# Norm factors from one product of ones with the summed squares, with the root taken on all partitions

## The chip, the cores and the metric

The kernel runs on one core of a Trainium2 chip. The metric is device time in microseconds of one execution, the median over several runs of the same program.

## The reference, cut to what matters

The reference is two layers of a diffusion block on 256 tokens of x and 256 context tokens, with 1024 channels. Every layer does a half feed-forward (ffn1), a mixing part (mix) and another half feed-forward (ffn2); the context leaves the last layer after mix's projections. Each of the three begins with a norm over the channels, and a last norm follows the second layer.

```python
def rms_norm(x, g):
    xf = x.astype(jnp.float32)
    y = xf * lax.rsqrt(jnp.mean(xf * xf, axis=-1, keepdims=True) + EPS)
    return (y * g.astype(jnp.float32)).astype(x.dtype)

def modulate(h, shift, scale):
    return h * (1 + scale) + shift

def half_ffn(h, shift, scale, gate, g, wi, wo):
    return h + 0.5 * gate * swiglu(modulate(rms_norm(h, g), shift, scale), wi, wo)
```

The convolution branch of mix has a layer norm over its 256 channels, which takes a sum of squares and a root in the same way.

## The kernel before, in words

Everything stays in fp32. A weight product of two fp32 matrices is written as three products of rounded parts (mm3, L177 to L179): high by high, high by low and low by high. So each weight tile `raw` that a DMA brings is split into `whi` (a cast on ScalarE, L165) and `wlo` (the difference on VectorE, L166), and each activation into a high part (`yh`, `hh`, `mh`) and a low part (`yl`, `hl`, `ml`). There are two buffers each of whi and wlo, and four PSUM tiles (`psm`) for the weight products and four (`psa`) for the small ones.

x lies in eight tiles of 128 channels by 512 tokens, of which columns 0 to 255 are x and 256 to 511 the context. The channels are on partitions, so a norm's sum over channels is a sum over partitions and over the eight tiles. It is made up of these steps:

- sumsq: ScalarE squares a tile of x (L374), VectorE adds it to the running sum `ss` (L378). The eighth tile's square is kept by itself.
- rstd: for each 128 tokens two fp32 products with `mean` as the moving side (L391 with ss, L392 with the last square) put the mean on the partitions, one column for each 128 tokens. An fp32 product shows as two records in the profile. rsqrt_cols (L204 to L215) takes the root of these columns with three Newton steps on VectorE.
- spread and bcast: VectorE multiplies the identity with each column (`diag`, L225), and a product with `ones` (L227) puts the factor of every token on all partitions, in a psa tile.
- norm_scale (L416) makes `ny` from x, the gain and that psa tile; norm_shift adds the shift on ScalarE, which gives yh (L423), and makes yl on VectorE (L424).

The output projection of each part ends in `project`. Where x and the context are both there, its last two output tiles (m = 6 and 7) are held back and then done by token halves: tile 6 first half, tile 7 first half, tile 6 second half, tile 7 second half. Each ends in x's update (L479) and sumsq. During the second half, hooks put rstd of the first half (at RA eighths of the products of tile 6) and its spread (at RB eighths of tile 7) among the weight products, so that the next part's norm of the first half is under way while TensorE works. There are four such places, with 256 tokens in each half.

In the last layer's ffn2 only x is left. There the first two weight pairs are multiplied with x times the gain, before the norm's factor is known (`z`), and late_act (L541) multiplies the results by the factor `rb` afterwards (zg at L544, zv at L546), which frees their psm tiles.

A tile scheduler sets the order of each engine's instructions from priorities, which follow the order of the code, and from a model of when operands are ready; each engine then works through its list in order. The start of the program (up to the first weight products) is ordered by the code as written. Waits between engines are by semaphore.

## Time and profile before

| what | value |
|---|---|
| runs | 1703.88, 1705.18, 1705.04 us (median 1705.04) |
| profiled execution, its own time | 1703.85 us |
| its span | 1702.1 us |
| mean granted TensorE clock | 0.997 of full speed |
| TensorE busy | 1678.8 us (99%) |
| VectorE busy | 1193.8 us (70%) |
| ScalarE busy | 575.8 us (34%) |

The span runs from the first to the last instruction of the profiled execution. A busy share says how much of the span an engine had an instruction in work. TensorE's instructions are pipelined: a product of 128x256 is recorded with 0.28 us, but at full clock they start 0.12 us apart. The granted clock is the share of full speed that the throttle gave TensorE. In the rows an engine, a line of the kernel and the operation are followed by what is written and what is read, without buffer numbers, and in brackets by the idle time before it and what ended that.

### The profile page before, as it was taken

How to read it: one execution, taken by the hardware profiler on the slowest of the kernel's cores; microseconds unless marked ns; L12 is line 12 of the kernel's file. 1: busy time of each engine (PE TensorE's matmuls, PEld its weight loads, DVE VectorE, ACT ScalarE, POOL GpSimd, SP SyncE). 2: the span in 40 equal slices, each digit the busy share in tenths (PEclk: the TensorE clock that was granted, in tenths of full speed). 3: DMA queues.
4: the chain of work that ended last, by engine and by line, in shares of the span. 5: the costliest groups of instructions: out<-in, count | busy, mean ns of one | idle time of the engine just before them, and what ended most of it. 6: DMA issues, size and time to landing. Idle time of an engine off the chain costs nothing.

```text
span 1702.1 us, 23539 instructions
## 1 busy us (share of the span) xinstructions
PE 1678.8 (99%) x9650; PEld 1440.4 (85%) x9650; DVE 1193.8 (70%) x2077; ACT 575.8 (34%) x737; POOL 33.6 (2%) x59
## 2 busy tenths in 40 slices
PE   8999999999999999999999999999999998999998
PEld 5888888878888898888888898888878897899998
DVE  5799866896675678888669776654464678775555
ACT  3322212333532443222122242221233254554343
POOL 0000000010000000000000000000000000000010
PEclk9999999999999999999999999999999999999999
DMA  9555644533232235545445425444433234344552
GB/s 370 185 188 182 211 157 153 180 121 104 102 105 85 95 129 180 183 163 183 166 148 193 165 104 194 166 155 149 151 124 106 86 130 162 110 157 177 179 195 79
DMA packets 51452, 262.55 MB, mean 154 GB/s; under 512 B 6010, under 2 KB 10944, under 8 KB 28816
## 3 DMA queue, kind: packets, MB, share of 16 engines
q1 hardware_dynamic: 49968, 257.05, 42.9%
q0 software_dynamic: 1376, 4.00, 0.6%
q8 instruction: 75, 1.23, 0.3%
q14 instruction: 33, 0.27, 0.0%
HBM read 257.88 MB, written 3.15 MB: 153 GB/s over the span
## 4 chain that ended last, share of the span: by engine, by line
PE 92%; DVE 3%; DMA 2%; ACT 1%; issue 1%; SPq 0%; POOL 0%; DVEq 0%; ACTq 0%; POOLq 0%
PE psm L177 29%; PE psm L178 28%; PE psm L179 28%; DVE acc L316 1%; ACT whi L165 1%; DVE wlo L166 1%; DMA adaw<-in_ada_w_dram 1%; DMA pm<-in_k_pool_dram 1%; PE psa L979 1%; DMA vec<-in_vecs_dram 1%; PE psa L1216 0%; PE psa L1038 0%; PE psa L1198 0%; PE psa L331 0%; PE psa L881 0%
## 5 line engine op out<-in xcount | busy, mean ns | idle before, releaser
L179 PE MATMUL psm<-yh,wlo 128*128 128x512 f32 (+1 forms) x1616 | 570.1, 354 | 2.5 <-DVE wlo L166 2.5
L177 PE MATMUL psm<-yh,whi 128*128 128x512 f32 (+1 forms) x1616 | 570.3, 355 | 1.4 <-DVE glu L776 0.9
L178 PE MATMUL psm<-yl,whi 128*128 128x512 f32 (+1 forms) x1616 | 571.1, 354 | 0.1
L165 ACT CAST whi<-raw 128x2048 fp32r<-128x2048 f32 (+3 forms) x172 | 304.1, 1770 | 599.8 <-PE psm L178 534.6
L166 DVE TENSOR_TENSOR wlo<-raw,whi 128x2048 fp32r<-128x2048 f32 (+3 forms) x172 | 363.7, 2116 | 133.6 <-ACT whi L165 133.3
L179 PEld LDWEIGHTS psm<-yh,wlo 128*128 128x128 f32 x1616 | 305.5, 189 | 46.5 <-DVE wlo L166 4.0
L177 PEld LDWEIGHTS psm<-yh,whi 128*128 128x128 f32 x1616 | 304.6, 189 | 46.3 <-issue 3.1
L178 PEld LDWEIGHTS psm<-yl,whi 128*128 128x128 f32 x1616 | 305.7, 189 | 42.5 <-DVE yl L424 0.9
L316 DVE SCALAR_TENSOR_TENSOR acc<-adaw,cvec,acc 128x512 f32<-128x512 f32 x392 | 274.5, 746 | 2.8
L177 PE MATMUL psm<-hh,whi 128*128 128x512 f32 (+1 forms) x752 | 265.1, 353 | 0.0
L179 PE MATMUL psm<-hh,wlo 128*128 128x512 f32 (+1 forms) x752 | 264.4, 352 | 0.0
L178 PE MATMUL psm<-hl,whi 128*128 128x512 f32 (+1 forms) x752 | 264.3, 351 | 0.0
L178 PEld LDWEIGHTS psm<-hl,whi 128*128 128x128 f32 x752 | 142.3, 189 | 19.4 <-DVE hl L166 0.4
L179 PEld LDWEIGHTS psm<-hh,wlo 128*128 128x128 f32 x752 | 142.3, 189 | 19.4 <-DVE acc L316 0.8
L177 PEld LDWEIGHTS psm<-hh,whi 128*128 128x128 f32 x752 | 142.2, 189 | 18.7 <-issue 0.2
L496 DVE TENSOR_TENSOR sg<-psm,sg 128x512 f32<-128x512 f32 (+1 forms) x90 | 54.3, 605 | 133.6 <-PE psm L179 119.6
L479 DVE SCALAR_TENSOR_TENSOR x<-psm,gt,x 128x256 f32<-128x256 f32 x112 | 50.4, 478 | 115.9 <-PE psm L179 115.8
L495 ACT ACTIVATE sg<-psm 128x512 f32<-128x512 f32 (+1 forms) x90 | 47.9, 532 | 215.7 <-PE psm L179 215.7
L374 ACT ACTIVATE sq<-x 128x512 f32<-128x512 f32 (+1 forms) x64 | 33.2, 523 | 90.9 <-DVE x L479 74.7
L177 PE MATMUL psm<-whi,yh 128*128 128x256 f32 (+1 forms) x200 | 58.1, 295 | 0.6 <-ACT whi L165 0.6
L178 PE MATMUL psm<-wlo,yh 128*128 128x256 f32 (+1 forms) x200 | 58.1, 294 | 0.0
L179 PE MATMUL psm<-whi,yl 128*128 128x256 f32 (+1 forms) x200 | 57.9, 293 | 0.0
(287 smaller groups left out, 1480.9 us busy)
## 6 DMA issues: line engine op xcount, KB each, us to landing
raw<-in_ffn_wi_dram SPq DMA_DIRECT2D x88, 1024.0 KB, 4.8
adaw<-in_ada_w_dram SPq DMA_DIRECT2D x66, 1024.0 KB, 5.1
raw<-in_ffn_wo_dram SPq DMA_DIRECT2D x32, 896.0 KB, 4.6
raw<-in_ffn_wo_dram SPq DMA_DIRECT2D x16, 1024.0 KB, 5.0
raw<-in_w_in_dram SPq DMA_DIRECT2D x14, 1024.0 KB, 4.8
raw<-in_w_out_dram SPq DMA_DIRECT2D x8, 1024.0 KB, 4.9
adaw<-in_ada_w_dram SPq DMA_DIRECT2D x24, 256.0 KB, 7.2
pm<-in_k_pool_dram SPq DMA_DIRECT2D x12, 256.0 KB, 3.1
```

The costliest lines, as they stand in the source:

```text
L165: self.nc.scalar.copy(hi[:, s], src[:, s])
L166: self.nc.vector.tensor_tensor(lo[:, s], src[:, s], hi[:, s].bitcast(F32), op=ALU.subtract)
L177: mm(ps, lhsT=ah, rhs=bh, start=first, stop=False)
L178: mm(ps, lhsT=ah, rhs=bl, start=False, stop=False)
L179: mm(ps, lhsT=al, rhs=bh, start=False, stop=last)
L316: nc.vector.scalar_tensor_tensor(acc, ws[half][:, k, :], sc, acc, op0=ALU.mult, op1=ALU.add)
L374: nc.scalar.activation(sq, self.x[m][:, lo:lo + n], AF.Square)
L479: nc.vector.scalar_tensor_tensor(self.x[m][:, s], ps[:, v * S - lo:v * S - lo + S], gate[v][:, m:m + 1], self.x[m][:, s], op0=ALU.mult, op ...
L495: nc.scalar.activation(sg, w[2][:, s], AF.Silu)
L496: nc.vector.tensor_tensor(sg, w[3][:, s], sg, op=ALU.mult)
L979: nc.tensor.matmul(ps[par], lhsT=fwd[:, 2 * i + par, :], rhs=cur[par], start=True, stop=True)
```

## The change

The eighth square is now added to ss like the others. For each half of 256 tokens one fp32 product of ones with ss puts the sum on all partitions, in a psa tile of 128x256. The root is then taken on that tile by eleven operations on VectorE, of which the last writes the factor back into the psa tile. Column products, diagonals and the products that spread them are gone from these norms; the last norm of the program keeps its columns, with one product for each 128 tokens. The factor no longer holds the square root of 1024, so the norms' gains are multiplied by it once at the start. The ones product of a first half is issued in the hook at RA; the hook at RB is gone, and the second half's follows its last weight product. In the convolution branch the two squares are added on VectorE, and one column product for each 128 tokens is left of two.

```diff
--- before.py
+++ after.py
@@ -35,7 +35,7 @@
 PRE = 400
 FSPLIT = 14
 F0 = (2.0, 0, 0.8, 16)
-RA, RB = 2, 4
+RA = 2
 PZ = 2
 F1 = (1.9, 0, 1)
 F2 = (0.8, 0, 1.0, 20)
@@ -240,6 +240,7 @@
                 v[name] = vt[:, l, at:at + c]
                 at += c
             self.vec.append(v)
+        self.norms = vt[:, :, 72:96]
 
 
     def ada_init(self, craw):
@@ -374,30 +375,37 @@
         nc.scalar.activation(sq, self.x[m][:, lo:lo + n], AF.Square)
         if m == 0:
             self.ss, self.rb = sq, {}
-        elif m < KT - 1:
+        else:
             nc.vector.scalar_tensor_tensor(self.ss[:, lo:lo + n], sq, EPS * D / P if m == 1 else 0.0, self.ss[:, lo:lo + n],
                                            op0=ALU.add, op1=ALU.add)
-        else:
-            self.last_sq = sq
 
     def rstd(self, lo, n):
 
         nc = self.nc
-        sq = self.last_sq
         nt = n // P
         ps = self.pa((P, nt, 2))
         for j in range(nt):
             a = lo + j * P
-            nc.tensor.matmul(ps[:, j, :], lhsT=self.ss[:, a:a + P], rhs=self.mean, start=True, stop=False)
-            nc.tensor.matmul(ps[:, j, :], lhsT=sq[:, j * P:j * P + P], rhs=self.mean, start=False, stop=True)
+            nc.tensor.matmul(ps[:, j, :], lhsT=self.ss[:, a:a + P], rhs=self.mean, start=True, stop=True)
         self.r = self.rsqrt_cols(ps, nt)
         return self.r
 
-    def spread(self, lo, r):
-
-        for i in range(r.shape[1] * P // S):
-            c = i * S // P
-            self.rb[lo // S + i] = self.bcast(r[:, c:c + S // P], S // P)
+    def spread(self, lo, n):
+
+
+        nc = self.nc
+        for v in range(lo // S, (lo + n) // S):
+            ps = self.pa((P, S))
+            nc.tensor.matmul(ps, lhsT=self.ones, rhs=self.ss[:, v * S:v * S + S], start=True, stop=True)
+            t = self.tmp((P, 2, S), name="root")
+            a, y = t[:, 0, :], t[:, 1, :]
+            nc.vector.tensor_single_scalar(a.bitcast(I32), ps.bitcast(I32), 1, op=ALU.logical_shift_right)
+            nc.vector.tensor_scalar(y.bitcast(I32), a.bitcast(I32), -1.0, float(0x5F3759DF), op0=ALU.mult, op1=ALU.add)
+            for i in range(3):
+                nc.vector.tensor_tensor(a, y, y, op=ALU.mult)
+                nc.vector.scalar_tensor_tensor(a, a, -0.5, ps, op0=ALU.mult, op1=ALU.mult)
+                nc.vector.scalar_tensor_tensor(ps if i == 2 else y, a, 1.5, y, op0=ALU.add, op1=ALU.mult)
+            self.rb[v] = ps
 
     def norm(self, l, name, T):
         yh = [self.yp.tile([P, T], F32R, tag="y", name=self.nm("yh")) for _ in range(KT)]
@@ -452,19 +460,11 @@
         elif m == KT - 2:
             self.held = (m, wh, wl, act, gate)
         else:
-            state = {}
-
-            def stats():
-                state["r"] = self.rstd(0, S)
-
-            def spread():
-                self.spread(0, state["r"])
-
             self.part(*self.held, 0, S, 3)
             self.part(m, wh, wl, act, gate, 0, S, 3)
-            self.part(*self.held, S, S, 3, {len(act) * RA // 8: stats})
-            self.part(m, wh, wl, act, gate, S, S, 3, {len(act) * RB // 8: spread})
-            self.spread(S, self.rstd(S, S))
+            self.part(*self.held, S, S, 3, {len(act) * RA // 8: lambda: self.spread(0, S)})
+            self.part(m, wh, wl, act, gate, S, S, 3)
+            self.spread(S, S)
 
     def part(self, m, wh, wl, act, gate, lo, w, last, hooks={}):
         nc = self.nc
@@ -480,10 +480,10 @@
                                            self.x[m][:, s], op0=ALU.mult, op1=ALU.add)
         if last:
             self.sumsq(m, lo, w)
-            if m == KT - 1 and last < 3:
-                r = self.rstd(lo, w)
-                if last == 1:
-                    self.spread(lo, r)
+            if m == KT - 1 and last == 1:
+                self.spread(lo, w)
+            elif m == KT - 1 and last == 2:
+                self.rstd(lo, w)
 
     def up_tiles(self, T):
         wh, wl = self.whl((P, 2 * KT, P))
@@ -921,17 +921,16 @@
         for i in range(2):
             nc.tensor.matmul(mu, lhsT=self.ones, rhs=cacc[i], start=i == 0, stop=i == 1)
         yield
-        sqs = []
+        sqs = self.tmp((P, T), name="css")
         for i in range(2):
             nc.vector.scalar_tensor_tensor(cacc[i], mu, -1.0 / DG, cacc[i], op0=ALU.mult, op1=ALU.add)
-            sq = self.tmp((P, T), name="csq")
+            sq = sqs if i == 0 else self.tmp((P, T), name="csq")
             nc.scalar.activation(sq, cacc[i], AF.Square)
-            sqs.append(sq)
+        nc.vector.tensor_tensor(sqs, sqs, sq, op=ALU.add)
         n = T // P
         ps = self.pa((P, n))
         for j in range(n):
-            for i in range(2):
-                nc.tensor.matmul(ps[:, j:j + 1], lhsT=sqs[i][:, j * P:(j + 1) * P], rhs=self.ones[:, 0:1], start=i == 0, stop=i == 1)
+            nc.tensor.matmul(ps[:, j:j + 1], lhsT=sqs[:, j * P:(j + 1) * P], rhs=self.ones[:, 0:1], start=True, stop=True)
         yield
         rb = self.bcast(self.rsqrt(ps, n, 1.0 / DG), n)
         for i in range(2):
@@ -1271,7 +1270,7 @@
             self.warm_up()
             for m in range(KT):
                 self.sumsq(m, 0, 512)
-            r = self.rstd(0, 512)
+            self.spread(0, 512)
             yh = [self.yp.tile([P, 512], F32R, tag="y", name=self.nm("yh")) for _ in range(KT)]
             yl = [self.yp.tile([P, 512], F32R, tag="y", name=self.nm("yl")) for _ in range(KT)]
             up = [self.up_tiles(512) for _ in range(2)]
@@ -1300,8 +1299,8 @@
                 self.split(up[i][0][:, half[p]], up[i][1][:, half[p]], raws[i][:, half[p]])
 
             acc = [self.pa() for _ in range(2)]
+            nc.vector.tensor_scalar(self.norms, self.norms, D ** 0.5, None, op0=ALU.mult)
             self.gemv(ws[2], every, acc[0])
-            self.spread(0, r)
             self.ada_end(0, 2, self.ada_row(acc[0]))
             self.derive(0, [1], two, 0, 4)
             scale(first)
```

The scheduler sets new orders with this. VectorE at B, the place where layer 0's mix ends and its ffn2 begins (about 616 to 622 us), before; sm, diag and psa_5218 belong to the root of the first half, x_113 to x_120 are the eight tiles of x, wlo is the low part of ffn2's second weight tile:

```order
L215 SCALAR_TENSOR_TENSOR sm_903_5178<-sm_902_5177,sm_901_5172 128x1
L225 TENSOR_SCALAR diag_5219<-ident_99,sm_903_5178 128x128 x2
L378 SCALAR_TENSOR_TENSOR sq_4920<-sq_5202,sq_4920 128x256
L416 SCALAR_TENSOR_TENSOR ny_5290<-x_113,gs_2817,psa_5218 128x256
L416 SCALAR_TENSOR_TENSOR ny_5294<-x_114,gs_2817,psa_5218 128x256
L416 SCALAR_TENSOR_TENSOR ny_5298<-x_115,gs_2817,psa_5218 128x256
L424 SCALAR_TENSOR_TENSOR yl_5282<-ny_5290,mods_197,yh_5274 128x256
L479 SCALAR_TENSOR_TENSOR x_120<-psm_5205,mods_197,x_120 128x256
L416 SCALAR_TENSOR_TENSOR ny_5302<-x_116,gs_2817,psa_5218 128x256
L166 TENSOR_TENSOR wlo_5365<-raw_5370,whi_5364 128x1024
```

and at the same place now, where root and psa_5085 are the first half's root and psa_5150 the second half's sums; the new lines L402 to L407 are the root, L379 is the sum of squares and L424 is norm_scale:

```order
L379 SCALAR_TENSOR_TENSOR sq_4850<-sq_5118,sq_4850 128x256
L406 SCALAR_TENSOR_TENSOR root_5087<-root_5087,psa_5085 128x256
L407 SCALAR_TENSOR_TENSOR root_5087<-root_5087 128x256
L405 TENSOR_TENSOR root_5087<-root_5087 128x256
L479 SCALAR_TENSOR_TENSOR x_120<-psm_5121,mods_197,x_120 128x256
L406 SCALAR_TENSOR_TENSOR root_5087<-root_5087,psa_5085 128x256
L166 TENSOR_TENSOR wlo_5255<-raw_5260,whi_5254 128x1024
L407 SCALAR_TENSOR_TENSOR psa_5085<-root_5087 128x256
L379 SCALAR_TENSOR_TENSOR sq_4850<-sq_5147,sq_4850 128x256
L424 SCALAR_TENSOR_TENSOR ny_5180<-x_113,gs_2790,psa_5085 128x256
L424 SCALAR_TENSOR_TENSOR ny_5184<-x_114,gs_2790,psa_5085 128x256
L402 TENSOR_SCALAR root_5152<-psa_5150 128x256
```

The norm_scales stood ahead of x_120 and of the split of wlo; now they stand behind both, and the root's last operation stands behind the split.

TensorE at B now, from the last weight product of the held tiles (mh by wlo) on; yh_5164 is the first of ffn2's eight yh tiles:

```order
L179 MATMUL psm_5121<-mh_4813,wlo_5015 128x256
L399 MATMUL psa_5150<-sq_4850,ones_100 128x256
L177 MATMUL psm_5246<-yh_5164,whi_5244 128x256
L177 MATMUL psm_5247<-yh_5164,whi_5244 128x256
L177 MATMUL psm_5256<-yh_5164,whi_5254 128x256
L177 MATMUL psm_5257<-yh_5164,whi_5254 128x256
L178 MATMUL psm_5246<-yl_5172,whi_5244 128x256
```

Behind the second half's ones product the list goes on with products that all read yh, as it did before behind a column product of the second half.

VectorE at E, the norm ahead of the last layer's ffn2 (about 1511 us), before; psm_12493 and psm_12494 hold the results of the first unscaled weight pair, wlo_12744 belongs to a later weight tile:

```order
L424 SCALAR_TENSOR_TENSOR yl_12457<-ny_12483,mods_198,yh_12449 128x256
L424 SCALAR_TENSOR_TENSOR yl_12458<-ny_12487,mods_198,yh_12450 128x256
L544 TENSOR_TENSOR zg_12592<-psm_12493,rb_12518 128x256
L546 TENSOR_TENSOR zv_12593<-psm_12494,rb_12518 128x256
L166 TENSOR_TENSOR wlo_12744<-raw_12749,whi_12743 128x2048
```

and now, where L432 is norm_shift's low part:

```order
L424 SCALAR_TENSOR_TENSOR ny_12276<-x_120,gs_9892,psa_12194 128x256
L166 TENSOR_TENSOR wlo_12533<-raw_12538,whi_12532 128x2048
L432 SCALAR_TENSOR_TENSOR yl_12245<-ny_12268,mods_198,yh_12237 128x256
L544 TENSOR_TENSOR zg_12381<-psm_12282,rb_12307 128x256
L432 SCALAR_TENSOR_TENSOR yl_12246<-ny_12272,mods_198,yh_12238 128x256
L546 TENSOR_TENSOR zv_12382<-psm_12283,rb_12307 128x256
```

The split moved from behind zg and zv to ahead of both.

## Rows read from the trace of the kernel before

**Rows 1.** The page, busy time: engine, us (share of the span), instructions.

```profile
PE 1678.8 (99%) x9650; PEld 1440.4 (85%) x9650; DVE 1193.8 (70%) x2077; ACT 575.8 (34%) x737; POOL 33.6 (2%) x59
```

**Rows 2.** Windows A and B: us; busy PE, PEld, DVE, ACT, POOL; clock; DMA.

```profile
410.00:422.00 12.00, 11.10 (x75) 10.48 (x73) 10.11 (x35) 5.92 (x11) 1.19 (x3) 0.86 0.31 105
618.00:630.00 12.00, 11.94 (x98) 11.50 (x97) 11.40 (x38) 6.42 (x12) 0.00 (x0) 1.00 0.00 1
```

**Rows 3.** Timeline of TensorE at B: start, us, engine, instruction.

```profile
613.68 0.38 PE L392 MATMUL psa<-mean,sq 128*128 128x2 f32 x2
...
614.38 0.36 PE L178 MATMUL psm<-ml,whi 128*128 128x256 f32 x1
...
617.57 0.61 PE L227 MATMUL psa<-diag,ones 128*128 128x128 f32 x4
617.93 0.36 PE L177 MATMUL psm<-mh,whi 128*128 128x256 f32 x1
...
619.60 0.48 PE L177 MATMUL psm<-yh,whi 128*128 128x256 f32 x2
```

**Rows 4.** Timelines of ScalarE (first row) and VectorE at B.

```profile
613.21 0.42 ACT L374 ACTIVATE sq<-x 128x256 f32<-128x256 f32 x1 [0.95 <-DVE x L479]
...
614.55 0.16 DVE L204 TENSOR_SCALAR sm<-psa 128x2 int32<-128x2 int32 x1 [1.43 <-PE psa L392]
...
618.22 1.26 DVE L416 SCALAR_TENSOR_TENSOR ny<-x,gs,psa 128x256 f32<-128x256 f32 x3 [0.26 <-PE psa L227]
...
620.62 1.22 DVE L166 TENSOR_TENSOR wlo<-raw,whi 128x1024 fp32r<-128x1024 f32 x1
```

**Rows 5.** Groups of TensorE: instructions | busy us, mean ns | idle before.

```profile
L934 PE MATMUL psa<-ones,csq 128*128 128x1 f32 x24 | 2.9, 240 | 0.0
...
L650 PE MATMUL psa<-abs,ones 128*128 128x256 f32 x8 | 2.6, 404 | 0.0
```

**Rows 6.** Groups of VectorE, shapes apart.

```profile
L314 DVE TENSOR_SCALAR acc<-adaw,cvec 128x512 f32<-128x512 f32 x56 | 26.1, 480 | 0.0
...
L652 DVE TENSOR_SCALAR rinv<-psa 128x256 f32<-128x256 f32 x4 | 1.7, 424 | 2.3 <-PE psa L650 2.3
```

**Rows 7.** Timeline of VectorE, two operations of which the second needs the first.

```profile
1284.81 0.42 DVE L682 TENSOR_TENSOR sp<-sp,psa 128x256 f32<-128x256 f32 x1 [3.23 <-ACT sp L681]
1285.27 0.42 DVE L684 TENSOR_TENSOR sp<-sp,psa 128x256 f32<-128x256 f32 x1
```

**Rows 8.** Windows of one microsecond at A.

```profile
414.00:415.00 1.00, 0.96 (x7) 0.96 (x7) 1.00 (x2) 1.00 (x3) 0.00 (x0) 0.78 0.00 0
415.00:416.00 1.00, 1.00 (x6) 1.00 (x6) 1.00 (x6) 0.19 (x1) 0.00 (x0) 0.50 0.00 0
...
417.00:418.00 1.00, 1.00 (x6) 1.00 (x6) 1.00 (x6) 0.51 (x1) 0.00 (x0) 0.52 0.85 344
```

**Rows 9.** Timelines of TensorE and VectorE at A.

```profile
411.77 0.36 PE L177 MATMUL psm<-yh,whi 128*128 128x256 f32 x1
...
412.89 2.33 DVE L166 TENSOR_TENSOR wlo<-raw,whi 128x1152 fp32r<-128x1152 f32 x2
...
414.92 0.56 PE L177 MATMUL psm<-yh,whi 128*128 128x256 f32 x1
```

**Rows 10.** Timelines of VectorE, ScalarE and TensorE at E.

```profile
1511.42 0.42 DVE L544 TENSOR_TENSOR zg<-psm,rb 128x256 f32<-128x256 f32 x1
1511.61 1.91 ACT L165 CAST whi<-raw 128x2048 fp32r<-128x2048 f32 x1 [0.37 <-ACT rb L563]
1511.75 0.41 DVE L546 TENSOR_TENSOR zv<-psm,rb 128x256 f32<-128x256 f32 x1
1511.89 0.39 PE L177 MATMUL psm<-yh,whi 128*128 128x256 f32 x1 [0.25 <-DVE zg L544]
...
1513.55 2.29 DVE L166 TENSOR_TENSOR wlo<-raw,whi 128x2048 fp32r<-128x2048 f32 x1 [1.38 <-ACT whi L165]
```

**Rows 11.** Timeline of VectorE at the start.

```profile
34.51 0.23 DVE L293 TENSOR_TENSOR mods<-psa,vec 128x4 f32<-128x4 f32 x2 [5.72 <-PE psa L291]
```

## The prediction

> **What bounds the kernel now.** The busy shares come first: TensorE works for 99% of the span, VectorE for 70% [rows 1]. So a product that leaves TensorE is worth its own time, and work on VectorE costs nothing until TensorE waits for it. Windows over the places where a norm ends one product and starts the next come second. At four of them the last two output tiles are done half by half: A at 410 us (ffn1 to mix, layer 0), B at 618 (mix to ffn2), C at 986 (ffn2 to ffn1 of layer 1), D at 1360 (ffn1 to mix, layer 1). At B TensorE is busy for 11.94 of 12 us at full granted clock; at A, where a longer weight split is in the way, for 11.10 at 0.86 [rows 2]. C reads like B, D like A. A fifth norm, E (mix to ffn2, layer 1), stands at 1496 to 1512: there the first two weight pairs work on unscaled x, and the scale is put on their results.
>
> Third, the timelines of B, where the reader is to see how a norm is hidden. TensorE's last column product for the first half is through at 614.38 [rows 3]; VectorE starts the root at 614.55 and the norm_scales at 618.22, after the diagonals and their products [rows 4]. TensorE meanwhile works on the second half of the held tiles and takes its first product with yh at 619.60 [rows 3]. The norm's chain takes 3.7 us and its cover is about 5 us; what the change does to these two numbers decides.
>
> **Removed and added on TensorE.** Of a half's eight records of column products at B, the last six run from 613.68 to 614.38, 0.70 us, which is 0.93 for eight at that pace; the first two are issued ahead among weight products, so I take 0.85. Its diagonal products hold TensorE from 617.57 to 617.93, 0.36 us [rows 3]. In their place comes one fp32 product of 128x256: L650's eight records, two for each product, take 2.6 us [rows 5], so 0.65. Net -0.55 per half. In the conv branch half of L934's 2.9 us goes [rows 5], and one 256-wide add on VectorE comes: -1.2, bounds -1.5 and 0.
>
> **The root.** Before, L204 to L215 work on two columns. Now eleven operations work on 128x256, each on the result of the one before. The nearest rows: a 256-wide operation that reads PSUM takes 424 ns [rows 6]; two that depend on each other start 0.46 us apart [rows 7]; two that don't, 0.33 apart (zg to zv) [rows 10]. L403, one integer input, isn't shown; L314, one input of 512 columns, takes 480 ns [rows 6], and half of that and the dependent price are its bounds: I take 0.32. With the others at 0.45 the chain is 4.8 us, between 3.6 (all at 0.33) and 5.1 (all at 0.46). I take the dependent price because every operation waits for its predecessor.
>
> **B, step by step.** The last square of the first half ends at 613.63 [rows 4]; its add (0.42, a third of three norm_scales' 1.26 [rows 4]) ends at 614.1, the ones product at 614.75. Ten root operations follow (4.4 us), and between them VectorE's list has three others (x of the last two tiles, one square's add, 0.4 each): 620.4. Then the weight split L166 stands ahead of the last root operation, where before four norm_scales stood ahead of it. It takes 1.22 [rows 4]: 621.6. The last root operation, a square's add and the first norm_scale end at 622.7, ScalarE's yh at 623.25, and the first product with yh starts at 623.3 instead of 619.60 [rows 3]. Nothing can fill the gap: the next rows on TensorE's list all read yh, and behind them stands all the rest. That is +3.7. Off it goes what the second half no longer does behind that point, 0.85 + 0.4 (its ones product falls into the wait): +2.45.
>
> **The clock.** At A the profile shows what a hold-up brings. TensorE is stopped there for a moment by the long split, and the granted clock is 0.78 in the microsecond from 414 and 0.52 in that from 417 [rows 8], with 0.50 between: half speed (1.2 GHz) from about 414.6 to 417.95, while TensorE was busy with six records in each microsecond. Half of these 3.35 us is lost, 1.7. At B nothing of the kind was there before [rows 2], and a wait of 4 us (619.1 to 623.3), longer than A's, now comes. I add 1.7: B +4.1, and C the same. The Trainium skill has this as a rule (TensorE: Matmul & The Clock Gate, Part 1): an array left idle falls to 1.2 GHz and must be busy for a while before it has 2.4 again. It speaks against this change, and A's rows agree; were the wait alone the price, the sum below would be 5 us less.
>
> **A and D.** The same list, with two splits of together 2.33 us [rows 9]: first product with yh at about 416.25 instead of 411.77. But before did little from there: three products with yh and two behind the first cast, 0.9 us, and its next block came at 414.92 [rows 9], with the slow clock behind it. So 416.25 - 414.92, plus 0.9 that is now still to do, less the second half's diagonals with their gaps (0.5): +1.7 each; the clock falls in both kernels.
>
> **E.** VectorE's list now has zg of the first unscaled pair behind the split of a later weight tile. zg frees the PSUM tile for TensorE's next product, which started at 1511.89, after a wait of 0.25 for it [rows 10]. Now the cast on ScalarE (1.91) starts when the second unscaled pair is done, about 0.65 sooner than 1511.64; then the split of 2.29 [rows 10], one norm_shift and zg: 1511.0 + 1.9 + 0.1 + 2.3 + 0.8 = 1516.1. That is +4.2, and with the clock +5.9.
>
> **The rest.** At the start the roots and the scaling of the gains are some 4.5 us more on VectorE, which idles for 5.72 us before 34.51, behind them [rows 11]. I take that idle time as their cover: 0, and +4.5 if the work that ends it is late by as much. The final norm keeps its columns, has one add in front and two products fewer: +0.25.
>
> **Sum** on the profiled run (1703.85 us, 1.75 of it around the span): 2 x 4.1 + 2 x 1.7 + 5.9 - 1.2 + 0.25 = +16.55, or 1720.4. The median of the runs shown, 1705.04, is 1.2 above that run: 1721.5.
>
> **Rivals.**
> 1. The other side. The products that go are the gain and the roots stay hidden: eleven halves at -0.55 and -1.2 in the conv branch, -7, so 1698. For it: TensorE at 99%. It turns on one number: at B the time from the sums (614.75) to yh must stay under the 4.4 us until the second half's products end at 619.1. Against it: at the lowest price the root is 3.6, and a norm_scale, yh and the split come on top. Steps under 0.28 us and a split behind the last of them would be needed.
> 2. The waits come, the clock does not fall for B, C and E: -5.1, 1716.5. For it: at E TensorE's wait of 0.25 left no mark. Against it: A.
> 3. The slow clock lasts twice as long at all five places, since the second half's eleven root operations stand among the first half's norm_scales and may break the stretch again (twelve products are 1.5 us of TensorE, 98 records in 12 us [rows 2], one norm_scale and shift 0.8 of VectorE): + 5 x 1.7, 1730.
> 4. Waits and gains cancel: within 0.2% (3.4 us, about what a measurement of this kernel tells from no change), 1705. It needs the split to move behind the root and E's wait to vanish.
>
> **Chances.** Forecast 0.62, rival 2 0.14, rival 3 0.10, rival 1 0.08, rival 4 0.06. The range goes down to rival 2 with roots at the independent price (1.2 us at each of five places, and the conv branch at its best): 1709; up to rival 3 and the start's bound in part: 1731. Faster is rival 1, 0.08; same rival 4 and a little of rival 2's lower end, 0.07; slower 0.85.
>
> **What would show it.** In the profile after: L402 to L407 in steps of 0.45; at B and C TensorE without work for about 4 us and a granted clock near 0.8 in the window that had 1.00; the split between the last two root operations; at E zg behind the split. The forecast is wrong, and rival 1 right, if the steps are near 0.3 or TensorE is still busy for 11.9 us of the window at B; rival 2 is right if TensorE waits and the clock stays at 1.00.

## The result, and the profile after

The changed kernel takes 1722.37 us (median of 4 runs, 1722.09 to 1723.12) against 1704.59 for the kernel before: the ratio is 1.0102, 95% interval 1.009 to 1.0114. It is slower by 17.8 us. Forecast were 1721.5. The total is right, in part because errors cancel; of the reasons behind it, the price of the slow clock was wrong and the one for E was half of the story. The experiments show both.

The profile after. Its page, busy times and the chain that ended last (for the first see [rows 1]):

```profile
PE 1678.8 (98%) x9524; PEld 1434.8 (83%) x9524; DVE 1220.0 (71%) x2028; ACT 576.3 (33%) x737; POOL 33.6 (2%) x59
...
PE 89%; DVE 6%; DMA 2%; ACT 2%; issue 1%; SPq 0%; DVEq 0%; ACTq 0%
```

TensorE's busy time is the same to a tenth although 126 records are gone, and the span is 18.6 us longer: some of its work ran at half speed, and for some microseconds it stood still. What it waited for (total us, times, longest), the first two lines of its list of waits:

```profile
PE psa L399 <- DVE sq L379: 14.5, 6, 4.2
PE psm L177 <- DVE zg L544: 5.0, 1, 5.0
```

Neither stood in the list of before. The first is the second half's ones product at A (4.16), B (2.95), C (2.95) and D (4.16), which waits for the last square's add; the second is E. The root's operations:

```profile
L405 DVE TENSOR_TENSOR root<-root 128x256 f32<-128x256 f32 x33 | 13.9, 422 | 0.7
...
L407 DVE SCALAR_TENSOR_TENSOR psa<-root 128x256 f32<-128x256 f32 x11 | 4.7, 426 | 0.1
...
L402 DVE TENSOR_SCALAR root<-psa 128x256 int32<-128x256 int32 x11 | 4.6, 421 | 4.5 <-PE psa L399 4.5
...
L403 DVE TENSOR_SCALAR root<-root 128x256 int32<-128x256 int32 x11 | 3.2, 290 | 0.2
```

They last 0.42 us each and 0.29 for L403. The timeline of VectorE at B shows the steps of 0.46 and 0.32, and the weight split between the last two root operations:

```profile
617.50 0.42 DVE L402 TENSOR_SCALAR root<-psa 128x256 int32<-128x256 int32 x1 [0.79 <-PE psa L399]
617.96 0.29 DVE L403 TENSOR_SCALAR root<-root 128x256 int32<-128x256 int32 x1
618.28 0.43 DVE L405 TENSOR_TENSOR root<-root 128x256 f32<-128x256 f32 x1
...
622.25 0.41 DVE L406 SCALAR_TENSOR_TENSOR root<-root,psa 128x256 f32<-128x256 f32 x1
622.64 1.22 DVE L166 TENSOR_TENSOR wlo<-raw,whi 128x1024 fp32r<-128x1024 f32 x1
623.79 0.43 DVE L407 SCALAR_TENSOR_TENSOR psa<-root 128x256 f32<-128x256 f32 x1
624.12 0.42 DVE L379 SCALAR_TENSOR_TENSOR sq<-sq,sq 128x256 f32<-128x256 f32 x1
624.46 0.86 DVE L424 SCALAR_TENSOR_TENSOR ny<-x,gs,psa 128x256 f32<-128x256 f32 x2
```

Where before had 3.67 us from the first root operation to the first norm_scale [rows 4], it is 6.96 now. TensorE at B, and one-microsecond windows of the same place (us; busy PE, PEld, DVE, ACT, POOL; granted clock; DMA):

```profile
624.60 0.70 PE L399 MATMUL psa<-sq,ones 128*128 128x256 f32 x2 [2.95 <-DVE sq L379]
625.53 0.74 PE L177 MATMUL psm<-yh,whi 128*128 128x256 f32 x4 [0.23 <-ACT yh L431]
```

```profile
622.00:623.00 1.00, 0.00 (x0) 0.00 (x0) 1.00 (x3) 1.00 (x3) 0.00 (x0) 1.00 0.00 0
...
627.00:628.00 1.00, 1.00 (x6) 1.00 (x6) 1.00 (x4) 0.49 (x1) 0.00 (x0) 0.50 0.00 0
...
629.00:630.00 1.00, 1.00 (x8) 1.00 (x8) 1.00 (x4) 0.00 (x0) 0.00 (x0) 0.68 0.00 0
```

The reader is to see three things: nothing on TensorE at 622, half the clock behind the wait, and VectorE at 1.00 in every row. The third is the one that the forecast used only in a rival. At E, ScalarE, VectorE and TensorE (before: [rows 10]):

```profile
1522.68 1.90 ACT L165 CAST whi<-raw 128x2048 fp32r<-128x2048 f32 x1 [0.96 <-PE psm L178]
...
1524.61 2.29 DVE L166 TENSOR_TENSOR wlo<-raw,whi 128x2048 fp32r<-128x2048 f32 x1 [0.70 <-ACT whi L165]
...
1524.90 0.35 ACT L563 COPY rb<-psa 128x256 f32<-128x256 f32 x1
...
1527.22 0.42 DVE L544 TENSOR_TENSOR zg<-psm,rb 128x256 f32<-128x256 f32 x1
...
1527.69 0.58 PE L177 MATMUL psm<-yh,whi 128*128 128x256 f32 x1 [4.97 <-DVE zg L544]
```

To put the loss down to places, each weight split (wlo) and each activation product (sg) of a kernel was set beside the same one of the kernel before; its start less the one of before is the shift there. The step of a place is the median shift behind it less the one ahead of it, in us, one profiled execution of each kernel; E's is taken from the splits just ahead of it (1480 to 1494), behind layer 1's convolution branch:

| kernel | start | A | B | C | D | E | median of runs |
|---|---|---|---|---|---|---|---|
| changed | 1.85 | 1.66 | 3.25 | 4.23 | 1.47 | 6.86 | 1722.4 |
| e_zg | 1.69 | 1.91 | 3.08 | 3.10 | 1.89 | 4.88 | 1721.7 |
| e_rb | 1.27 | 1.75 | 3.05 | 3.08 | 1.89 | 2.93 | 1717.3 |
| e_order | 1.17 | 1.52 | 2.95 | 2.95 | 1.54 | 7.63 | 1720.8 |
| e_two | 2.54 | 0.46 | 4.34 | 4.36 | 0.93 | 6.44 | 1720.9 |
| e_clock | 1.68 | 2.03 | 5.97 | 5.99 | 2.00 | 6.71 | 1728.7 |
| e_half | 3.41 | 2.17 | 3.89 | 2.76 | 1.92 | 6.31 | 1722.7 |
| e_clock1 | -0.06 | 2.00 | 2.86 | 2.92 | 1.96 | 6.57 | 1721.5 |
| e_both | 2.54 | 0.05 | 1.72 | 1.74 | 0.28 | 7.45 | 1715.9 |
| e_cols | 3.48 | -0.72 | 3.81 | 3.82 | 0.07 | 0.21 | 1711.3 |
| e_win | 1.80 | 0.16 | 0.51 | 0.49 | 1.63 | 0.19 | 1704.2 |
| e_sqrt | 1.32 | 3.04 | 5.55 | 5.27 | 2.11 | 1.46 | 1725.4 |
| e_conv | 3.15 | -1.47 | 0.00 | -0.02 | -1.52 | 0.00 | 1702.8 |

Two places stand between these. Where the convolution branch of layer 0 is (between the splits at 565 and 590), the changed kernel gains 0.89, and so does every other kernel of the table. Where layer 1's is (1449 to 1481), it gains 0.40 and e_conv 0.30, the others between 0 and 0.72; ahead of that, from 1418 to 1426, the changed kernel loses 0.34, of which the cause was not followed up.

One execution is not the next, and this has to be kept in mind with every step. e_zg and e_rb have the changed kernel's code and lists at A to D, and there C's step is 3.1 in both and not 4.23. The kernels from e_zg to e_both but e_two have the changed kernel's start, and e_conv has that of the kernel before, yet their starts lie between -0.06 and 3.41, and 3.15. That goes with the clock of the single execution: over 24 to 48 us it is 1.00 in the kernel before and in e_clock1 (start -0.06), 0.93 in the changed kernel and e_zg (1.85, 1.69) and 0.86 in e_half and e_conv (3.41, 3.15).

### The profile page after: what moved, and what is told of

It is laid out like the page before. It is cut to its first block, busy times and chain, and to the rows that moved or that the text cites. A ratio compares the mean times of both kernels' runs of the same rounds, so it can differ in the third digit from the quotient of the medians.

```text
span 1720.7 us, 23239 instructions
## 1 busy us (share of the span) xinstructions
PE 1678.8 (98%) x9524; PEld 1434.8 (83%) x9524; DVE 1220.0 (71%) x2028; ACT 576.3 (33%) x737; POOL 33.6 (2%) x59
## 3 DMA queue, kind: packets, MB, share of 16 engines
HBM read 257.88 MB, written 3.15 MB: 152 GB/s over the span
## 4 chain that ended last, share of the span: by engine, by line
PE 89%; DVE 6%; DMA 2%; ACT 2%; issue 1%; SPq 0%; DVEq 0%; ACTq 0%
PE psm L177 28%; PE psm L178 28%; PE psm L179 28%; DVE wlo L166 1%; DVE acc L317 1%; ACT whi L165 1%; DMA adaw<-in_ada_w_dram 1%; DMA vec<-in_vecs_dram 1%; PE psa L1037 0%; PE psa L1215 0%; PE psa L978 0%; DMA pm<-in_k_pool_dram 0%; PE psa L399 0%; PE psa L1197 0%; PE psa L332 0%
```

## The experiments

**E alone.** e_zg holds VectorE's order at E, e_rb also ScalarE's:

```diff
 def up(f, pieces=1):
     w = self.up_tiles(T)
-    self.split(w[0], w[1], self.load(wi[f]), pieces)
+    with self.after({**self.late[0], **self.copied} if early and f > 2 else {}):
+        self.split(w[0], w[1], self.load(wi[f]), pieces)
```

Here `late[0]` is VectorE's zv of the first unscaled pair, `copied` is ScalarE's copy of rb (e_rb only), and `after` queues the block's instructions behind them on the same engine.

> The changed kernel with one edit: in the last layer's ffn2 the split of the fourth weight tile is queued on VectorE behind zv of the first unscaled pair, so zg comes first, as before the change. Theory (zg behind the split stops TensorE at E, the wait 5.0 us and the half clock behind it): about 6.9 us of the 17.8 come back, 1715.5 us, no wait of TensorE for zg over 0.5 us and a granted clock of 1.00 from 1518 to 1537. Rival (TensorE would there wait for the weight tile or for yl instead, so the wait only changes its name): 1721 to 1723.

> The changed kernel with its orders at E as before the change, on both engines: on ScalarE the copy of the norm factor (rb) stands ahead of the cast of the fourth weight tile, on VectorE zg and zv ahead of its split. In e_zg, with VectorE's order alone, zg waited for rb, which stood behind the cast. Theory (the cast of 1.9 us and the split of 2.3 in a row are E's price, with the half clock behind the wait): the shift between the two kernels' rows over E falls from 6.85 us to about 0.5, 1716 us or 2 below e_zg. Rival (E's norm is late by itself, as the root on VectorE ends 2.4 us later than before): it falls to 3 only.

e_zg: 1721.71 us, ratio to before 1.0101 (1.0084 to 1.0118); TensorE still waits 3.2 us for zg. ScalarE in e_zg says why:

```profile
1522.28 1.90 ACT L165 CAST whi<-raw 128x2048 fp32r<-128x2048 f32 x1 [0.96 <-PE psm L178]
...
1524.49 0.35 ACT L566 COPY rb<-psa 128x256 f32<-128x256 f32 x1
```

zg needs rb, and rb's copy stands behind the cast. E's step falls by 2.0. e_rb: 1717.34, ratio 1.0076 (1.006 to 1.0091), with rb ahead of the cast:

```profile
1522.26 0.37 ACT L566 COPY rb<-psa 128x256 f32<-128x256 f32 x1 [0.46 <-DVE ny L424]
1522.88 0.42 DVE L546 TENSOR_TENSOR zg<-psm,rb 128x256 f32<-128x256 f32 x1
...
1523.35 0.39 PE L177 MATMUL psm<-yh,whi 128*128 128x256 f32 x1 [2.38 <-DVE zg L546]
```

E's step falls from 6.86 to 2.93, to the rival's 3 and not to the theory's 0.5: two orders, on two engines, make 3.9 us of it. The rest is put down to a norm that is late by itself, which no kernel tests alone.

**The split between the root's operations.** e_order queues the split at A to D behind the third norm_scale:

```diff
+            with self.after(self.behind if pieces > 1 else {}), self.prio(-PRE if pieces > 1 else 0):
                 self.nc.vector.tensor_tensor(lo[:, s], src[:, s], hi[:, s].bitcast(F32), op=ALU.subtract)
```

> The changed kernel with one edit: at the four half-by-half boundaries the weight split that stood between the last two root operations is queued on VectorE behind the third norm_scale. Theory (VectorE's list with the root, the split and the norm_scales in a row is what TensorE waits for): the waits shrink by the split's length, 1.2 us at B and C and 2.3 at A and D, 7 us in all: 1715.4 us, and down to 1709 if shorter waits leave the clock up. Rival (TensorE needs the split's low part as soon as yh, so its products with wlo wait instead): 1720 to 1726.

1720.76, ratio 1.0095 (1.008 to 1.011). The four steps together fall from 10.6 to 9.0 (e_zg and e_rb, with the split in its old place, have 10.0 and 9.8), not by 7. The first yh comes sooner and later ones come late: in e_order TensorE waits 6.5 us for yh, in six pieces. The place of the split was not the price, and the time is in the rival's range.

**A shorter root.** e_two has two Newton steps:

```diff
-            for i in range(3):
+            for i in range(2):
```

> The changed kernel with two Newton steps in the root in place of three (the third step is left out, so the norm factors are less exact): eight operations in the chain instead of eleven, 1.37 us less, and the scheduler then puts the weight split behind the root and the norm_scales at B. Theory (the root's length on VectorE goes one to one into TensorE's wait): at B and C the wait falls from 3.9 to about 1 us and the clock stays up, 4.5 us each; A and D 3 to 4 each, the start 1.5: 1705 to 1710. Rival (TensorE's waits come from elsewhere, or something else is late next): 1718 to 1723.

1720.9, ratio 1.0096 (1.0079 to 1.0112): in the rival's range and not the 1705 to 1710 of the theory. At A and D the steps fall by 1.2 and 0.5, at B they rise by 1.1. At B and C the scheduler put the second piece of the split behind all norm_scales, a second difference, and e_cols and e_win below show that this one alone costs 3.3 us at each of the two.

**The clock alone, and VectorE's work alone.** e_clock keeps TensorE busy in the wait; e_half leaves the second half's root out:

```diff
             self.part(m, wh, wl, act, gate, S, S, 3)
-            self.spread(S, S)
+            with self.after(self.mark(mybir.EngineType.PE)):
+                ps = self.pa((P, P))
+                for i in range(16):
+                    self.nc.tensor.matmul(ps, lhsT=self.ones, rhs=self.ones, start=True, stop=True)
+                with self.after(self.mark(mybir.EngineType.PE)):
+                    self.spread(S, S)
```

```diff
+            if lo:
+                self.rb[v] = self.rb[0]
+                continue
             t = self.tmp((P, 2, S), name="root")
```

> The changed kernel with one edit: at the four half-by-half boundaries 16 products of ones with ones (128x128, result unused) stand on TensorE's list between the last held weight product and the second half's ones product, that is in the wait. Theory (the wait lets the clock fall, and the half-speed stretch behind it is a price of its own): with the clock at 1.00 through and behind the wait, the lost time by the windows' granted clocks, (1 - 0.77) x 15 at A and C and (1 - 0.89) x 15 at B and D, comes back, 10 us: 1712; by the forecast's 1.7 for each of four places, 1715.6. Rival (the slow stretch has another cause, the wait is the whole price): 1722 or somewhat above.

> The changed kernel without the root of the second half at the four half-by-half boundaries; the context tokens there take the factors of the first half's tokens (the roots left out are the second half's alone, its sums are still made and waited for). The first half's chain keeps its eleven operations and, by the order of VectorE's list, the split in front of the last. Theory T (VectorE is busy without a gap from the sums to the last norm_scale, and its whole work there paces TensorE): B and C lose most of their 3.3 and 4.4 us, 1715 us. Theory L (the forecast's: the time to the first yh and the clock behind it are the price): the first half's chain is as long as before, 1721 to 1723.

e_clock: 1728.72, ratio 1.0143 (1.0127 to 1.0159), slower than the changed kernel although its clock stays up. e_half: 1722.74, ratio 1.0107 (1.0094 to 1.0121), as the changed kernel. By e_half theory T fell, by e_clock the forecast's price for the clock. But e_clock's lists differ at B and C as e_two's do, and e_half's there have the split's second piece further ahead, behind the third norm_scale. At A and D the splits stand in all of them where they do in the changed kernel. So the pair was run again in one order.

At B the record has a plainer case against that price. The changed kernel and e_zg have the same code and the same lists there; in the one execution the clock fell behind the wait, in the other it did not (columns as in [rows 2], the changed kernel first):

```profile
618.00:634.00 16.00, 12.82 (x89) 12.07 (x88) 15.82 (x42) 6.34 (x12) 0.00 (x0) 0.89 0.01 2
```

```profile
618.00:634.00 16.00, 12.57 (x99) 11.62 (x97) 15.79 (x42) 6.25 (x12) 0.00 (x0) 1.00 0.01 2
```

The steps are 3.25 and 3.08 (e_rb, also at 1.00: 3.05), so this fall cost 0.2 us and not 1.7. VectorE was full in both. At C the fall lasted longer in the changed kernel than in e_zg (granted clock 0.79 and 0.89 over 990 to 1006), and there the steps are 4.23 and 3.10: a longer fall has a price.

**Both together.** e_both has both edits, e_clock1 the products alone, and both queue the second piece of the split ahead of the second half's norm_scales at B and C (the branch for these tiles; all others are split as before):

```diff
+                self.split(w[0][:, :KT], w[1][:, :KT], raw[:, :KT])
+                nc.scalar.copy(w[0][:, KT:], raw[:, KT:])
+                with self.after(self.eighth), self.prio(-PRE):
+                    nc.vector.tensor_tensor(w[1][:, KT:], raw[:, KT:], w[0][:, KT:].bitcast(F32), op=ALU.subtract)
```

> e_clock and e_half together (16 products of ones with ones in each of the four waits, and no root of the second half, which takes the first half's factors), with the split's second piece at B and C ahead of the second half's norm_scales as in the changed kernel. Theory P (behind the first yh two limits run side by side, TensorE at half clock and VectorE's full list, so that taking away either alone gave nothing): with both away the boundaries cost only the wait for the first yh, some 2 us less at each of the four: about 1714 us. Theory L (the wait for the first yh alone is the price): 1722. If the products in the wait cost time by themselves, as e_clock's 1728.7 may be read: 1726 or above.

> e_clock with the split's second piece at B and C queued ahead of the second half's norm_scales, as in the changed kernel and in e_both: so it is e_both with the second half's root put back. Theory P (with the clock up, VectorE's full list is the limit behind the first yh): the steps at B and C come to the changed kernel's 3.3 to 4.2 us, from e_clock's 6.0, and 1.5 us or more above e_both's 1.7; A and D stay at 2.0: 1722 to 1724 us. Rival (the second half's root plays no part, e_both gained by the order alone): the steps at B and C come to 1.7, A and D to 0.1 to 0.3: 1716.

e_both: 1715.88, ratio 1.0064 (1.005 to 1.0078). e_clock1: 1721.47, ratio 1.0097 (1.0083 to 1.0111). Sixteen microseconds at A show it, first the changed kernel, then e_half, e_clock1 and e_both (columns as in [rows 2]):

```profile
412.00:428.00 16.00, 11.84 (x73) 11.00 (x72) 15.81 (x41) 7.24 (x14) 1.19 (x3) 0.79 0.23 80
```

```profile
413.70:429.70 16.00, 11.84 (x68) 10.92 (x67) 13.81 (x33) 8.89 (x19) 0.00 (x0) 0.79 0.23 76
```

```profile
412.00:428.00 16.00, 14.16 (x99) 12.32 (x98) 15.62 (x39) 7.33 (x19) 0.00 (x0) 1.00 0.22 75
```

```profile
412.00:428.00 16.00, 15.18 (x119) 14.35 (x117) 15.21 (x37) 9.29 (x19) 0.00 (x0) 1.00 0.22 76
```

With the root taken away, VectorE has 2 us free and TensorE's clock is as low as before the edit (0.79): nothing gained. With the clock at 1.00, VectorE is full (15.62), and TensorE waits for it behind the first yh, as e_clock1's waits in this window say (yh is made on ScalarE from ny, which comes from VectorE's list). e_clock1 is 1.9 us ahead of the changed kernel here; from 410.1 on its row has 15.85 for VectorE and the same clock.

```profile
PE psm L177 <- ACT yh L433: 1.3, 3, 0.5
PE psa L399 <- DVE sq L379: 0.6, 1, 0.6
```

With both, A's step is 0.05 and D's 0.28, from 2.0 and 2.0 with the clock alone and 2.2 and 1.9 with the root alone. The 16 products stand in e_both too, so it is not they that cost e_clock1 its 2 us. So behind the wait two limits run side by side, TensorE at half speed and VectorE's full list, of about the same length here; taking one away shows the other. That is theory P, and A and D show it. At B and C only part of P came: e_clock1's steps are 2.9 and e_both's 1.7, so the root does count with the clock up, but by 1.1 to 1.2 and not by the 1.5 or more that P asked for, and 2.9 is under its 3.3 to 4.2.

The 0.05 doesn't say that the wait is free. The kernel before ran at half the clock for a while at A and D itself [rows 8], and e_conv, whose clock stayed up there, is 1.5 us faster at each. Counted from a kernel with its clock up, e_both's wait costs about 1.5 at A and 1.8 at D, as the 1.7 at B and C, and the two limits together 1.2 to 1.6 more at each place of the changed kernel, 2.5 at C with its longer fall. These are estimates from the steps of single executions.

**Parts of the change on the kernel before.** e_cols takes the eighth add with half the column products, and the convolution branch, and keeps the narrow root and E's orders; e_win adds the second piece's place (as in e_both) and eight products at the start; e_conv has the convolution branch alone:

```diff
-            nc.tensor.matmul(ps[:, j, :], lhsT=self.ss[:, a:a + P], rhs=self.mean, start=True, stop=False)
-            nc.tensor.matmul(ps[:, j, :], lhsT=sq[:, j * P:j * P + P], rhs=self.mean, start=False, stop=True)
+            nc.tensor.matmul(ps[:, j, :], lhsT=self.ss[:, a:a + P], rhs=self.mean, start=True, stop=True)
```

> The kernel before with its column products, diagonals and narrow roots, and two parts of the change taken alone: the eighth square is added on VectorE, so a half has two column products instead of four, and the convolution branch has one column product for each 128 tokens instead of two; the orders at E are held as in the kernel before. Theory: TensorE loses 0.4 us a half and 0.8 to 1.2 in the convolution branch, 11 halves, 5 in all; VectorE gets one more 256-wide add a half, which at B and C, where it has no gap, gives 0.8 each back: 1700.5 us, below the kernel before (1704.0). Rival (the adds are hidden): 1699; rival (they stand in front of the root in a chain that has no room): 1704 or above.

> e_cols with two more edits: at B and C the second piece of the second weight tile's split is queued on VectorE behind the eighth norm_scale of the first half and ahead of the second half's, as in the kernel before (in e_cols it stood behind all norm_scales), and at the start eight products of ones with ones, result overwritten, fill TensorE's gap at 28 to 30 us. Theory (e_cols lost at B and C by that order, 2.1 us each and waits behind it, and at the start by the clock, 3.5 us): B and C come to -0.8 each, the start to 0, the convolution branch -0.8 and A, D, E near 0: 1701.5 us, below the kernel before (1704.5). Rival (the eighth add delays the second half's sums and TensorE waits all the same): 1707 or above; rival (the start's clock does not heed eight products): 1705.

> The kernel before with the convolution branch's part of the change alone (its two squares added on VectorE, one column product for each 128 tokens instead of two); the lists of the engines are else as before. Theory (the forecast's -1.2 us, 0.8 and 0.4 in the two layers): 1.0 to 1.4 us below the kernel before; by the rows of the changed kernel, where the shift falls by 0.9 in layer 0 and rises by 0.4 in layer 1, 0.5. Rival (TensorE has other work there, nothing is gained): no difference.

e_cols: 1711.28, ratio 1.0039 (1.0026 to 1.0051), 11 us above its theory: it lost 3.8 at B and at C with no wide root in it, and 3.5 at the start. The wait that ends the stretch there, TensorE in e_cols, and ten microseconds of e_cols and then of e_win:

```profile
638.80 0.50 PE L179 MATMUL psm<-yh,wlo 128*128 128x256 f32 x2 [0.52 <-DVE wlo L166]
```

```profile
634.00:644.00 10.00, 8.65 (x61) 7.42 (x61) 6.75 (x16) 3.75 (x8) 0.00 (x0) 1.00 0.30 105
```

```profile
634.00:644.00 10.00, 10.00 (x84) 9.94 (x83) 6.28 (x17) 6.00 (x11) 0.00 (x0) 1.00 0.08 34
```

In e_cols the split's second piece runs at 637.53 on VectorE, in e_win at 629.41. With that order set, e_win's steps at B and C are 0.5 (not the -0.8 that was expected) and its time is 1704.15, ratio 0.9989 (0.998 to 0.9998). e_conv: 1702.76, ratio 0.9986 (0.9977 to 0.9995). Both are below the kernel before by about 0.1%, their intervals overlap, and the rest of the change brought no gain beyond e_conv's in any form that was run. e_conv's own part is its 0.89 in layer 0 and 0.30 in layer 1, 1.2 together. Its profile's further gain at A and D (1.5 each) comes with a clock of 1.00 from 412 to 420, where the kernel before ran three microseconds at half speed [rows 8], and why that differs between two kernels with the same code there stays open.

**Another root.** e_sqrt takes ScalarE's square root, VectorE's reciprocal and one Newton step, with E's orders as in e_rb:

```diff
+            nc.scalar.activation(a, ps, AF.Sqrt)
+            nc.vector.reciprocal(y, a)
+            nc.vector.tensor_tensor(a, y, y, op=ALU.mult)
+            nc.vector.scalar_tensor_tensor(a, a, -0.5, ps, op0=ALU.mult, op1=ALU.mult)
+            nc.vector.scalar_tensor_tensor(ps, a, 1.5, y, op0=ALU.add, op1=ALU.mult)
```

> The changed kernel with a shorter root (ScalarE's square root from the psa tile, VectorE's reciprocal and one Newton step: four operations of VectorE instead of eleven) and the orders at E as in e_rb. Theory T and theory L both: VectorE has 5 us less to do at a boundary than with the long root, and the first yh comes 2 us sooner, so the boundaries cost nothing and the removed products show: 1700 to 1706. Rival (ScalarE now loads its function tables and does casts, yh and squares in one list, so yh waits there instead): 1710 or above.

1725.35, ratio 1.0124 (1.011 to 1.0138): the rival's side. At B ScalarE loads a table in front of the root, and VectorE's reciprocal is not an operation like the others:

```profile
618.39 1.28 ACT L402 ACT_TABLE_LOAD   x1 [1.29 <-PE psa L399]
619.69 0.39 ACT L402 ACTIVATE root<-psa 128x256 f32<-128x256 f32 x1
...
620.11 1.75 DVE L403 RECIPROCAL root<-root 128x256 f32<-128x256 f32 x1
```

The load takes 1.28 us and the reciprocal 1.75, as long as four of the operations that it stands in for. So a half's root is 1.5 us shorter on VectorE (3.0 us of operations against 4.5), not the 5 us a boundary that was expected, and the first half's chain is no shorter: 6.9 us from the start of the load (618.39) to the first norm_scale (625.31), against 6.96 in the changed kernel. Why its steps are above the changed kernel's, and why it loses 3.0 us between D and E, where no root stands, was not followed up.

## Why the prediction was right or wrong

- **The root's length: right.** The forecast took 0.45 and 0.32 a step; 0.46 and 0.32 were measured, and the split stood in front of the last operation. Ten operations and the three among them took 5.1 us (617.50 to 622.64), not 5.6: put between two dependent operations, such a one added 0.22 to 0.28 us and not the 0.4 that was booked.
- **The wait at B and C: right in size, the wrong instruction.** The forecast had TensorE without a weight product for 4.2 us until the first yh; it was 3.9 (621.65 to 625.53), of which 2.95 went to the sums of the second half, which stand ahead of yh on its list and whose add stands behind the same split, and 0.23 to yh. B's step is 3.25 and C's 4.23, against 4.1 for each; with 3.1 for both places in e_zg and e_rb, 4.1 was about 1 too high.
- **The clock as a price of its own: this step failed.** It added 1.7 us to the wait at B, C and E. In the changed kernel's profile the fall came (0.50 at 627), but at A, B and D it is no price to be added: at B the same lists with and without the fall give 3.25 and 3.08; e_clock1 had the clock at 1.00 and the steps of A and D did not fall, and e_both shows that there the clock counts once VectorE's list is shorter as well. Only the longer fall at C went with 1.1 us more; for E no run separates the clock. The forecast named the second half's root among the norm_scales only in rival 3, as something that might lengthen the slow stretch; it is a second limit about as long as that stretch. The term came out near its size since one of the two is paid in any case. The reading that it started from was wrong too: at A of the kernel before it was not VectorE's long split that held TensorE up; its two waits there were 0.29 us for ScalarE's cast and 0.61 for its square.
- **Rivals 2 and 3: each in part, and neither its price.** Rival 2 had the waits come and the clock stay up at B, C and E. At B that is what e_zg and e_rb show, without the 1.7 us that it would take off. Rival 3 had a slow stretch twice as long at all five places. Over 16 us the clock was 0.79 at A and C and 0.89 at B, so it came at A and C, and not with 1.7 more at A.
- **A and D: right in size**, 1.66 and 1.47 against 1.7, but the forecast made this of the late first yh alone. e_both has that wait too and a step of 0.05 with the clock up: counted from a clock that stays up, about half of the changed kernel's price is the pair of limits, and the kernel before paid for a slow clock there already.
- **E: 1.0 too low, half of the reason.** 6.86 against 5.9. The forecast saw the cast and the split ahead of zg, but not that rb, which zg needs, stands on ScalarE behind that cast; e_zg undid the split alone and got 2.0, e_rb both and got 3.9.
- **The convolution branch: right.** -1.2 was booked; the changed kernel's shift falls by 0.89 and 0.40, e_conv's by 0.89 and 0.30. The rise by 0.4 that e_conv's expectation speaks of is the loss at 1418 to 1426, ahead of that branch.
- **The start: right about the roots.** 0 was booked, the profile shows 1.85, with half the clock at 32 to 36 where before had 1.00; the same code gave -0.06 in e_clock1, with the clock at 1.00. So the 1.85 is the clock of that execution, which the forecast did not have there; why it falls in one and not in the other stays open. The window in the changed kernel:

```profile
32.00:34.00 2.00, 2.00 (x7) 0.36 (x4) 0.00 (x0) 0.36 (x1) 0.00 (x0) 0.58 1.10 416
```

- **The sum: in part luck.** For the profiled run it was 1720.4, and that took 1722.55. The start's 1.85 and E's 1.0 came on top, and 0.7 less at B and C and 0.3 less at A and D took some of it back. With C as in e_zg and e_rb, B and C together are 2 too high, which the unbooked clock at the start then hides.
- **Rival 1** (the products that go are the gain): e_cols took products away and left the root narrow, and was slower too, by list order; with that order set, e_win is 0.1% faster and not 7 us. Its point of decision was right for the changed kernel: the time from sums to yh, 8.0 us (617.5 to 625.5), is far over 4.4.

## What to carry to other kernels

Before work is moved from a busy engine to a second one, look whether the second one has gaps at that very place, not over the span: VectorE was busy for 70% of the span of the kernel before and 95% of the twelve microseconds at B [rows 2]. When one suspect is taken away and the time stays, take away two together before both are acquitted. And look at more than one execution of the same code before a step of a microsecond is put down to an edit. After any edit under a scheduler, compare the order of the untouched instructions on every engine: here the split's second piece was worth 3.3 us at each of B and C (e_cols and e_win), and a cast and a split at E 3.9.

## What the runs showed that was not expected

- A slow clock can be free, or nearly: at B a fall cost 0.2 us, and at A, where the clock was 0.79 over 16 us, restoring it gave nothing until VectorE's work was cut. It isn't always: e_conv gained 1.5 us at A with the clock up, on the kernel before with its short roots.
- A reciprocal of 128x256 on VectorE took 1.75 us, four times a multiplication of that size.
- The same instructions at the start took between -0.06 and 3.41 us more than in the kernel before, from one execution to the next, with the clock at 0.5 or 1.00 in the same microseconds.
- A clock fall came without a long stop: in the kernel before at A, where TensorE's longest wait was 0.61 us for ScalarE, with 0.44 busy in the microsecond ahead of the fall; e_conv had the clock at 1.00 there with 1.27 of 2 us busy at 416 to 418. And it stayed away behind a wait of 2.95 us, at B in e_zg. The first two (the kernel before, then e_conv):

```profile
413.00:414.00 1.00, 0.44 (x2) 0.21 (x2) 1.00 (x1) 1.00 (x3) 0.00 (x0) 1.00 0.00 0
```

```profile
416.00:418.00 2.00, 1.27 (x9) 1.04 (x9) 1.95 (x3) 2.00 (x6) 0.00 (x0) 1.00 0.00 0
```
